# Hybrid encoder layer on one core: casts of reloaded block sums placed behind a fixed ScalarE order, earlier squares and norms in the first FFN's opening, and unordered first weight casts in the second FFN

## Chip, cores and metric

One core of a Trainium2 chip. The metric is the device time of one execution of the whole program in microseconds (us); shorter is better. Before the change it is 1978.37 us, the median of three runs (1977.86 to 1978.83).

## What is computed

One layer of a bidirectional encoder on x of 1 x 1024 x 1024 float32: a half feed-forward step, a mixer (attention beside a recurrent branch), a second half step, a last norm.

```python
def swiglu_half_step(x, gain, w_in, w_out):
    h = rms_norm(x, gain)
    gate, up = jnp.split(h @ w_in, 2, axis=-1)
    return (jax.nn.silu(gate) * up) @ w_out
...
  x = x + 1/2 * SwiGLU_1(RMSNorm(x))
  x = x + W_out [ GroupNorm_attn(GQA(...)) || HGRN2_bidir(...) ]
  x = x + 1/2 * SwiGLU_2(RMSNorm(x))
  x = RMSNorm(x)
```

D_MODEL is 1024 and D_FF is 2816, so `w_in` is 1024 x 5632. The change lies wholly in the `h @ w_in` product of the two feed-forward steps, here called FFN1 and FFN2 ("ffn1" and "ffn2" in names).

## The kernel before, in words

**Precision and blocks.** A float32 operand is split in two: a part rounded to fp32r, written by ScalarE (the "cast"), and the remainder, written by VectorE or GpSimd (the "low" of a weight, the "rest" of an activation). Each product is three matmuls: rounded by rounded, rounded by rest, rest by rounded.

`ffn_up` makes one 128-wide column group f of `w_in` at a time, 22 in all (gate and up halves together). For f = 2 and on it uses a Strassen-like scheme over half blocks (`unit` and `product`, matmuls at L311, PSUM tiles pa, pb, pc, pd). The first two groups, f = 0 and 1, are done by plain products (`plain`, matmuls at L293, tiles pp), because those need only the transposed x (operands B1 and B2, made of B11, B12 and B21, B22), while the Strassen products need block sums T1 to T4 of the transposed x as well.

**Row blocks.** x is 8 tiles of 128 rows, two to a row block i = 0 to 3. In FFN1 the last four tiles share one large tile, x_late. For each block: squares and their sums (`square`, ScalarE), the root (`root`: VectorE, then GpSimd's pow), normalisation (`norm`, VectorE), 16 transposes (`turn`, PE at L467), four casts from PSUM into B (`cast`, ScalarE), four rests (`rest`, VectorE), then block sums t1 to t4 (`sum1`, `sum2`, `sums`), which become T operands. t1 is not transformed in place: it is stored to DRAM (d_t1) and reloaded (`load_sum`, tile t1b). The reloaded t1b is written into the space of B12 by `place` (cast at L185, rest at L186), once the plain products have read B12's columns there. `place` also writes the T2 to T4 pieces of blocks 2 and 3.

**What sets the order.** Each engine runs its own queue in order. FFN1's opening has its order written out by hand: `act`, `dve` and `pool` issue each instruction behind the last one of that engine that was given in this way (all of these appear at L412, the line of the helper). Code outside it is placed by a scheduler that knows dependencies and priorities. `self.behind(x)` keeps an instruction behind x; `self.exp`, set to the last hand-ordered ScalarE instruction, is used so for the weight splits (L93, L94) of the first units. PSUM tiles share eight banks (tag "u"), so a transpose or a product also waits until the last reader of its bank is done. SyncE (SP) issues loads and stores in its queue's order.

The opening runs: blocks 0 and 1 are transposed; `plain(0)` and `plain(1)` run on columns 0 to 128 (named pp_0_0 and pp_1_0), then 128 to 256 (pp_0_128, pp_1_128), with the transposes of block 1 between the halves of the second, block 2 before and block 3 between the halves of the fourth; then both run on columns 256 to 512 (96 matmuls) over all four blocks, and unit f = 2 follows.

**FFN2's opening** has no hand order. The last attention tile pair ends in two residual additions per x tile (L1269, after the scale rs_ao). x_6 is normalised on the chip and stored; x_7 is stored to DRAM (L1275, GpSimd) as soon as it is whole and reloaded (L1516, SP), squared (L115) and normalised. `blocks(0)` transposes and casts the first block, `first(0, ...)` splits the weights of f = 0 (cast at L402, low at L404), with both kinds kept behind the last cast and rest of block 0 (`since`, `lo_since`), and `first(1, ...)` likewise. raw_in tiles are raw weights (L249).

Of the kernel before, what the change touches and what calls it, by code (L numbers as in the profile page):

```python
# [44 lines left out]
class Trunk:  # L45
# [135 lines left out]
    def place(self, dst, pt, i, lo_engine):  # L181

        ptv = pt.rearrange("p (k t) -> p k t", t=P)
        hi, lo = (dst[:, j, :, i * P : (i + 1) * P] for j in range(2))
        self.cast = self.nc.scalar.copy(hi, ptv)  # L185
        self.lo = lo_engine.tensor_sub(lo, ptv, hi.bitcast(F32))  # L186

    def ffn_up(self, name, pair, acts, comb, early_lo, mid, early, begin):
# [21 lines left out]
        def both(row):  # L210

            key = f"B{row}"
            if key not in T:
                T[key] = self.B.tile([P, 2, 2, 4, 512], F32R, name=f"{name}_{key}", tag="B")
            return T[key]
# [60 lines left out]
        def result(what, nm):  # L276
            return self.cc.tile([P, 512], F32, name=f"{what}_{name}_{nm}", tag="c")

        def plain(f, A, lo, hi, act=lambda fn, *a: fn(*a), dve=lambda fn, *a: fn(*a), between=None):

            w = hi - lo
            if begin and w == P:
                shared = self.bank(f"pp_{name}_{f}_{lo}")
                ps = [shared[:, 0 : 2 * w], shared[:, 2 * w : 4 * w]]
            else:
                ps = [self.bank(f"pp{j}_{name}_{f}_{lo}") for j in range(2)]
            halves = lambda t: t[:, : 2 * w].rearrange("p (h t) -> p h t", h=2)
            B = [both(row) for row in "12"]
            for j in range(2):
                for k in range(NK):  # L290
                    ks = slice((k % 4) * P, (k % 4 + 1) * P)
                    for i, (a, b) in enumerate(((0, 0), (0, 1), (1, 0))):
                        nc.tensor.matmul(  # L293
                            halves(ps[j]), A[2 * j + k // 4][:, a, ks],
                            B[k // 4][:, :, b, k % 4, lo:hi],
                            start=(k == 0 and i == 0), stop=(k == NK - 1 and i == 2),
                        )
                if between and not j:
                    between()
            sg = result("sg", f"{f}_{lo}")  # L300
            act(nc.scalar.activation, sg[:, : 2 * w], ps[0][:, : 2 * w], AF.Silu)
            dve(nc.vector.tensor_mul, sg[:, : 2 * w], sg[:, : 2 * w], ps[1][:, : 2 * w])
            nc.sync.dma_start(
                acts[f].rearrange("p (h t) -> p h t", h=2)[:, :, lo:hi], halves(sg)
            )
# [88 lines left out]

        A, ahead = {}, {}

        def first(f, raws, since, lo_since):
            A[f] = []
            for i in range(4):
                hl = self.wop.tile([P, 2, 512], F32R, name=f"hl_in_{name}_{f}_A{i}", tag="wop")  # L400
                with self.behind(since):
                    nc.scalar.copy(hl[:, 0, :], raws[i])  # L402
                with self.behind(lo_since):
                    early_lo.tensor_sub(hl[:, 1, :], raws[i], hl[:, 0, :].bitcast(F32))  # L404
                A[f].append(hl)

        if begin:
# [11 lines left out]
            xs, gain, gain_ps, raws = begin(raw_weights, big)  # L419
# [5 lines left out]
            def square(t, on_act=True):  # L425
                out = ss[t // 2][:, t % 2 : t % 2 + 1]
                if on_act:
                    act(nc.scalar.activation, junk[0], xs[t], AF.Square, accum_out=out)
                else:
                    dve(nc.vector.scalar_tensor_tensor, out=junk[1], in0=xs[t], scalar=1.0, in1=xs[t],  # L430
                        op0=ALU.mult, op1=ALU.mult, accum_out=out)

            def root(i, j, n):
                work = self.stat.tile([P, 2, n], F32, name=f"rs_n0_{i}_{j}", tag=f"rs{n}")
                dve(nc.vector.tensor_scalar, work[:, 0, :], ss[i][:, j : j + n], 1.0 / D, EPS,
                    ALU.mult, ALU.add)
                pool(nc.gpsimd.tensor_tensor, out=work[:, 1, :], in0=work[:, 0, :],
                     in1=self.neg_half[:, :n], op=ALU.pow)
                for m in range(n):
                    rs[2 * i + j + m] = work[:, 1, m : m + 1]  # L440

            def norm(t, cols=slice(0, D)):
                dve(nc.vector.scalar_tensor_tensor, out=xs[t][:, cols], in0=xs[t][:, cols],
                    scalar=rs[t], in1=gain[:, cols], op0=ALU.mult, op1=ALU.mult)
# [26 lines left out]
            def parts(key, i):  # L471
                return (op(key)[:, j, :, i * P : (i + 1) * P] for j in range(2))

            def cast(key, pt, i):
                hi, lo = parts(key, i)
                act(nc.scalar.copy, hi, pt.rearrange("p (k t) -> p k t", t=P))
# [25 lines left out]
            def second():  # L502
                pt, t = turn(1), sum_tiles(1)
                for k in range(4):
                    cast(keys[k], pt[k], 1)
                for k in (0, 2, 1, 3):
                    rest(keys[k], pt[k], 1)
                square(4)
                square(5)
                return pt, t  # L510

            with self.tc.high_priority():
                square(0)
                square(1)
                root(0, 0, 1)
                norm(0, lower)
                root(0, 1, 1)
                norm(0, upper)
                norm(1, lower)
                norm(1, upper)  # L520
                pts = turn(0)
                casts, lows = weight(0, raws[0])
                casts[0]()
                casts[1]()
                for k in range(4):
                    cast(keys[k], pts[k], 0)
                casts[2]()
                casts[3]()
                lows[0]()
                rest("B11", pts[0], 0)  # L530
                rest("B12", pts[2], 0)
                lows[1]()
                rest("B21", pts[1], 0)
                rest("B22", pts[3], 0)
                lows[2]()
                lows[3]()
                square(2)
                square(3)
                casts, lows = weight(1, raws[1])
                for f in casts:  # L540
                    f()
                root(1, 0, 2)
                lows[0]()
                lows[1]()
                norm(2)
                norm(3)
                lows[2]()
                lows[3]()
                t0 = sum_tiles(0)
                sum1(0, t0, pts)  # L550
                plain(0, A[0], 0, 128, act, dve)
                turned = []
                plain(1, A[1], 0, 128, act, dve, lambda: turned.append(second()))
                ptn, t1_ = turned.pop()
                root(2, 0, 2)
                norm(4)
                norm(5)
                square(6)
                square(7)
                root(3, 0, 2)  # L560
                sum2(t0, pts)
                sum1(1, t1_, ptn)
                norm(6)
                norm(7)
                plain(0, A[0], 128, 256, act, dve)
                sum2(t1_, ptn)
                third = []

                def rows(i):
                    pt = turn(i)  # L570
                    for k in range(4):
                        cast(keys[k], pt[k], i)
                        rest(keys[k], pt[k], i)
                    third.append(pt)

                rows(2)
                plain(1, A[1], 128, 256, act, dve, lambda: rows(3))
                pts, ptn = third
                for key, t in zip(("T2", "T3"), t0[1:3]):
                    cast(key, t, 0)  # L580
            cast("T4", t0[3], 0)
            for i, t in ((0, t0), (1, t1_)):
                for key, src in zip(("T2", "T3", "T4"), t[1:]):
# [8 lines left out]
        else:  # L592
            with self.tc.high_priority():
                ahead[0] = pair(0)
                raws = raw_weights(0)
# [1 line left out]
            with self.tc.high_priority():  # L597
                banks = blocks(0)
            since, lo_since = self.cast, self.lo
            first(0, raws, since, lo_since)  # L600
            plain(0, A[0], 0, 128)
            sums(0, *banks)
            banks = blocks(1)
# [10 lines left out]
        for f in range(early, NF):  # L614
            u = unit(f)
            next(u)
            self.exp = None
            if before:
                next(before)
            next(u)  # L620
            before = u
            if f - early < early:
                stored_sums(f - early)
            if f == NF // 2 and mid:
                mid()
# [961 lines left out]
```

## Time and profile before

| | |
|---|---|
| median of three runs | 1978.37 us |
| the profiled execution | 1975.92 us |
| its span, first to last instruction | 1973.9 us |
| TensorE (PE) busy | 1938.7 us, 98% of the span |
| VectorE (DVE) busy | 1256.3 us, 64% |
| ScalarE (ACT) busy | 796.7 us, 40% |
| GpSimd (POOL) busy | 763.0 us, 39% |
| mean granted TensorE clock | 0.997 |

The page of the profile gives sums over the whole span. The timeline of an engine lists its instructions in order of time, runs of the same kind merged: start, duration, engine, line, operation, output<-inputs, count, and in brackets how long the engine had stood idle before and whose end released it. Names there leave buffer numbers out (t1b_ffn, pp_ffn). The windows view gives busy time per engine in chosen stretches, with the granted clock and the DMA engines' share. L numbers are those of the kernel before; after the change they are one higher from L185 on.

### The profile page before, as it was taken

The page shows a single profiled execution, that of the slowest core. Times are in us where ns is not written, and L with a number is a line of the kernel's source. Part 1 is how long each engine was busy: PE and PEld are TensorE (multiplying, and loading weights), DVE is VectorE, ACT ScalarE, POOL GpSimd, SP SyncE. Part 2 cuts the span into 40 slices and gives each one's busy share as a digit, 9 for nine tenths or more (in the row PEclk, how much of TensorE's full clock was granted, in tenths as well). Part 3 has the DMA queues.
Part 4 walks back from the last instruction along what each step waited for, and adds up shares of the span by engine and source line. Part 5 has one row for each costly group of instructions (what it writes and reads, how often), then busy time and mean ns, then how long its engine had stood idle before and what let it go on. Part 6 is the DMA issues. An engine that isn't in the chain of part 4 may idle for free.

```text
span 1973.9 us, 26682 instructions
## 1 busy us (share of the span) xinstructions
PE 1938.7 (98%) x10233; PEld 1663.8 (84%) x10233; DVE 1256.3 (64%) x1546; ACT 796.7 (40%) x1260; POOL 763.0 (39%) x581
## 2 busy tenths in 40 slices
PE   8999999999999999999999999989999999999998
PEld 7888888887888799989899888878888888888886
DVE  7556676656976672768772556666456666657866
ACT  6333343324444432333332446654333333344344
POOL 1764645534660000041230324425555455426711
PEclk9999999999999999999999999999999999999999
DMA  8333333227775211131224352175333333158644
GB/s 249 107 123 100 103 123 101 70 97 275 250 232 171 100 33 54 33 97 29 90 87 139 123 176 76 65 239 149 126 111 96 107 102 96 68 187 316 219 122 161
DMA packets 218011, 256.70 MB, mean 130 GB/s; under 512 B 12550, under 2 KB 148762, under 8 KB 217884
## 3 DMA queue, kind: packets, MB, share of 16 engines
q1 hardware_dynamic: 208684, 224.06, 35.4%
q0 software_dynamic: 9200, 30.94, 4.1%
q8 instruction: 80, 1.31, 0.3%
q14 instruction: 47, 0.39, 0.1%
HBM read 184.17 MB, written 70.78 MB: 129 GB/s over the span
## 4 chain that ended last, share of the span: by engine, by line
PE 88%; DVE 4%; DMA 3%; issue 2%; ACT 2%; POOL 0%; SPq 0%; DVEq 0%; POOLq 0%; ACTq 0%
PE pa_ffn L311 17%; PE pd_ffn L311 11%; PE pya_ffn L700 7%; PE rec_ps L162 6%; PE pc_ffn L311 6%; PE pb_ffn L311 6%; PE pp_ffn L293 4%; PE pye_ffn L700 3%; PE pyc_ffn L700 3%; PE pyd_ffn L700 3%; PE lv L928 3%; PE ri_ps L839 2%; PE aq_ps L839 2%; PE pa L1217 2%; PE pv L1189 2%; PE s L1157 2%
## 5 line engine op out<-in xcount | busy, mean ns | idle before, releaser
L311 PE MATMUL pa_ffn<-ffn_T,hl_in_ffn_S 128*128 128x512 f32 x960 | 236.7, 389 | 0.0
L94 DVE TENSOR_TENSOR hl_in_ffn_A<-raw_in_ffn,hl_in_ffn_A 128x512 fp32r<-128x512 f32 x120 | 173.0, 1442 | 93.7 <-ACT hl_in_ffn_A L93 93.6
L311 PE MATMUL pd_ffn<-ffn_B,hl_in_ffn_S 128*128 128x512 f32 x936 | 225.6, 389 | 0.0
L311 PEld LDWEIGHTS pa_ffn<-ffn_T,hl_in_ffn_S 128*128 128x128 f32 x960 | 180.2, 188 | 37.4
L311 PEld LDWEIGHTS pd_ffn<-ffn_B,hl_in_ffn_S 128*128 128x128 f32 x936 | 175.7, 188 | 36.5
L94 DVE TENSOR_TENSOR hl_in_ffn_S<-s_ffn,hl_in_ffn_S 128x512 fp32r<-128x512 f32 x160 | 140.7, 884 | 79.6 <-ACT hl_in_ffn_S L93 79.4
L93 ACT CAST hl_in_ffn_S<-s_ffn 128x512 fp32r<-128x512 f32 x160 | 99.1, 622 | 213.6 <-PE pd_ffn L311 160.3
L93 ACT CAST hl_in_ffn_A<-raw_in_ffn 128x512 fp32r<-128x512 f32 x120 | 75.0, 626 | 139.9 <-PE pc_ffn L311 70.9
L94 DVE TENSOR_TENSOR hl_out_ffn_A<-raw_out_ffn_A,hl_out_ffn_A 128x1024 fp32r<-128x1024 f32 (+1 forms) x66 | 97.6, 1493 | 50.8 <-ACT hl_out_ffn_A L93 50.2
L94 DVE TENSOR_TENSOR hl_out_ffn_S<-raw_out_ffn_S,hl_out_ffn_S 128x512 fp32r<-128x512 f32 (+1 forms) x88 | 106.3, 1217 | 36.8 <-ACT hl_out_ffn_S L93 36.8
L267 POOL TENSOR_TENSOR s_ffn<-s_ffn,raw_in_ffn 128x512 f32<-128x512 f32 x40 | 63.5, 1588 | 165.4 <-issue 110.5
L162 PE MATMUL rec_ps<-hm,hl_rec_w 128*128 128x512 f32 x528 | 121.6, 390 | 1.9 <-DVE hm L145 1.9
L700 PE MATMUL pya_ffn<-hl_out_ffn_S 128*128 128x512 f32 x528 | 120.7, 389 | 0.4 <-DVE hl_out_ffn_S L94 0.4
L162 PEld LDWEIGHTS rec_ps<-hm,hl_rec_w 128*128 128x128 f32 x528 | 98.7, 188 | 22.4 <-DVE hm L145 2.2
L700 PEld LDWEIGHTS pya_ffn<-hl_out_ffn_S 128*128 128x128 f32 x528 | 99.0, 188 | 21.4 <-DVE hl_out_ffn_S L94 0.8
L311 PE MATMUL pa_ffn<-ffn_B,hl_in_ffn_A 128*128 128x512 f32 x480 | 116.9, 389 | 0.0
L311 PE MATMUL pc_ffn<-ffn_T,hl_in_ffn_A 128*128 128x512 f32 x480 | 115.9, 389 | 0.0
L311 PE MATMUL pb_ffn<-ffn_B,hl_in_ffn_A 128*128 128x512 f32 x480 | 115.3, 389 | 0.0
L93 ACT CAST hl_out_ffn_S<-raw_out_ffn_S 128x512 fp32r<-128x512 f32 (+1 forms) x88 | 73.3, 837 | 96.4 <-PE pya_ffn L700 40.9
L266 POOL TENSOR_TENSOR s_ffn<-raw_in_ffn 128x512 f32<-128x512 f32 x40 | 52.6, 1316 | 138.4 <-DVE hl_in_ffn_S L94 138.2
L311 PEld LDWEIGHTS pc_ffn<-ffn_T,hl_in_ffn_A 128*128 128x128 f32 x480 | 90.1, 188 | 18.7
L311 PEld LDWEIGHTS pb_ffn<-ffn_B,hl_in_ffn_A 128*128 128x128 f32 x480 | 90.1, 188 | 18.7
(295 smaller groups left out, 4018.3 us busy)
## 6 DMA issues: line engine op xcount, KB each, us to landing
raw_in_ffn<-in_ffn_w_in SPq DMA_DIRECT2D x88, 512.0 KB, 4.2
raw_out_ffn_S<-d_comb SPq DMA_DIRECT2D x88, 256.0 KB, 2.7
d_comb<-g_ffn POOLq DMA_DIRECT2D x80, 256.0 KB, 2.3
raw_out_ffn_A<-d_act SPq DMA_DIRECT2D x66, 256.0 KB, 5.2
ffn_kept<-in_ffn_w_out SPq DMA_DIRECT2D x65, 256.0 KB, 5.3
d_act<-g_ffn SPq DMA_DIRECT2D x60, 256.0 KB, 2.2
raw_out_ffn_A<-in_ffn_w_out SPq DMA_DIRECT2D x52, 256.0 KB, 5.4
x<-d_x SPq DMA_DIRECT2D x24, 512.0 KB, 4.8
```

The costliest lines, as they stand in the source:

```text
L93: nc.scalar.copy(hl[:, 0, :], src)
L94: (lo_engine or nc.vector).tensor_sub(hl[:, 1, :], src, hl[:, 0, :].bitcast(F32))
L162: nc.tensor.matmul(out, hl[:, a, ks], h[half][b][:, k, cols], start=(k == 0 and i == 0), stop=(k == NK - 1 and i == 2),)
L266: nc.gpsimd.tensor_add(s1, a21, a22)
L267: nc.gpsimd.tensor_sub(s2, s1, a11)
L293: nc.tensor.matmul(halves(ps[j]), A[2 * j + k // 4][:, a, ks], B[k // 4][:, :, b, k % 4, lo:hi], start=(k == 0 and i == 0), stop=(k == NK ...
L311: nc.tensor.matmul(ps, A[:, a, ks], op(key)[:, b, k, :], start=(first and k == 0 and i == 0), stop=(k == 3 and i == 2), skip_group_check=True,
L700: nc.tensor.matmul(ps, hl[:, a, j * P : (j + 1) * P], hl[:, b, hi], start=(first and i == 0 and n == 0), stop=(i == last and n == 2), skip ...
L839: nc.tensor.matmul(ps[:, tt, :], h[half][a][:, k, ts], hl[k // 4][:, b, ws], start=(k == 0 and i == 0), stop=(k == NK - 1 and i == 2),)
L928: nc.tensor.matmul(pl[:, cs], now[:, 0, cs], now[:, 1, cs], start=True, stop=True)
L1157: nc.tensor.matmul(ps[:, ks], qT[:, a, qs], kT[:, b, kv, ks], start=(i == 0), stop=(i == 2))
L1189: nc.tensor.matmul(ps, vt[:, j, a, vs], pT[j][:, b, i4, :], start=(st == 0 and i == 0), stop=(st == NT - 1 and i == 2),)
```

## The change

Four edits, none of which adds or removes an instruction or changes a tile, a load or a matmul in size:

1. `place` issues its cast behind `self.exp`, and `self.exp` is cleared two calls later in the loop over units.
2. `first(0, ...)` in FFN2 no longer passes `since` and `lo_since`, so the f = 0 weight casts and lows are not tied to block 0. f = 1 still passes them.
3. The squares of x tiles 4 and 5 move ahead of `plain(1)` on columns 0 to 128; root 2, norms 4 and 5, squares 6 and 7 and root 3 move into `second()`, between that product's halves.
4. The casts of T2 and T3 of block 0 move from behind block 3's casts to between block 2 and block 3.

```diff
@@ place
-        self.cast = self.nc.scalar.copy(hi, ptv)
+        with self.behind(self.exp):
+            self.cast = self.nc.scalar.copy(hi, ptv)
...
@@ first
-        def first(f, raws, since, lo_since):
+        def first(f, raws, since=None, lo_since=None):
...
@@ second
                     rest(keys[k], pt[k], 1)
-                square(4)
-                square(5)
+                root(2, 0, 2)
+                norm(4)
+                norm(5)
+                square(6)
+                square(7)
+                root(3, 0, 2)
                 return pt, t
...
                 plain(0, A[0], 0, 128, act, dve)
+                square(4)
+                square(5)
                 turned = []
                 plain(1, A[1], 0, 128, act, dve, lambda: turned.append(second()))
                 ptn, t1_ = turned.pop()
-                root(2, 0, 2)
-                norm(4)
-                norm(5)
-                square(6)
-                square(7)
-                root(3, 0, 2)
                 sum2(t0, pts)
...
                 rows(2)
+                for key, t in zip(("T2", "T3"), t0[1:3]):
+                    cast(key, t, 0)
                 plain(1, A[1], 128, 256, act, dve, lambda: rows(3))
                 pts, ptn = third
-                for key, t in zip(("T2", "T3"), t0[1:3]):
-                    cast(key, t, 0)
...
-            first(0, raws, since, lo_since)
+            first(0, raws)
...
             u = unit(f)
             next(u)
-            self.exp = None
             if before:
                 next(before)
             next(u)
+            self.exp = None
```

**ScalarE in FFN1, around the transposes of block 3.** In a name such as pt_ffn1_B12_2 the digit after B12 is the row block; t1b_ffn1_0 is the reloaded sum of block 0; sg_ffn1_1_128 is the SiLU of pp_1_128. Before:

```order
L412 CAST ffn1_B1_281<-pt_ffn1_B12_2_547 128x4x128
L185 CAST ffn1_B1_281<-t1b_ffn1_0_800 128x4x128
L412 CAST ffn1_B2_283<-pt_ffn1_B22_2_552 128x4x128
L185 CAST ffn1_B1_281<-t1b_ffn1_1_802 128x4x128
L412 CAST ffn1_B1_281<-pt_ffn1_B11_3_590 128x4x128
L412 CAST ffn1_B2_283<-pt_ffn1_B21_3_595 128x4x128
L412 CAST ffn1_B1_281<-pt_ffn1_B12_3_600 128x4x128
L230 COPY t3_ffn1_2_662<-pt_ffn1_B12_2_547 128x512
L412 CAST ffn1_B2_283<-pt_ffn1_B22_3_605 128x4x128
L412 ACTIVATE sg_ffn1_1_128_642<-pp_ffn1_1_128_565 128x256
```

After, at the same place:

```order
L413 CAST ffn1_B1_281<-pt_ffn1_B12_2_547 128x4x128
L413 CAST ffn1_B2_283<-pt_ffn1_B22_2_552 128x4x128
L413 CAST ffn1_T2_191<-t2_ffn1_0_317 128x4x128
L413 CAST ffn1_T3_566<-t3_ffn1_0_318 128x4x128
L413 CAST ffn1_B1_281<-pt_ffn1_B11_3_593 128x4x128
L231 COPY t3_ffn1_2_662<-pt_ffn1_B12_2_547 128x512
L413 CAST ffn1_B2_283<-pt_ffn1_B21_3_598 128x4x128
L413 CAST ffn1_B1_281<-pt_ffn1_B12_3_603 128x4x128
L413 CAST ffn1_B2_283<-pt_ffn1_B22_3_608 128x4x128
L413 ACTIVATE sg_ffn1_1_128_645<-pp_ffn1_1_128_568 128x256
```

The two casts of t1b have left this stretch (they now stand behind the T casts that follow it and one weight cast), two T casts of block 0 have come in, and the copy of t3_2 stands behind one cast of block 3 where it stood behind three.

**VectorE at the start of FFN2.** rs_ao3 is the scale of the last attention pair, x2_6 and x2_7 the last two x tiles, hl_in_ffn2_0_A0 to A3 the split weights of f = 0. Before:

```order
L1205 TENSOR_TENSOR ssq3_10705<-ssq3_10705,sq3_3_11216 128x256
L85 TENSOR_SCALAR rs_ao3_11249<-oss3_11246 128x2
L1269 SCALAR_TENSOR_TENSOR x2_6_11219<-pa6_11221,rs_ao3_11249,x2_6_11219 128x512 x2
L1269 SCALAR_TENSOR_TENSOR x2_7_11263<-pa7_0_11265,rs_ao3_11249,x2_7_11263 128x512
L85 TENSOR_SCALAR rs_n2_6_11258<-ss_n2_6_11256 128x1
L125 SCALAR_TENSOR_TENSOR xn_n2_6_11255<-x2_6_11219,rs_n2_6_11258,g_ffn2_norm_9012 128x1024
L1269 SCALAR_TENSOR_TENSOR x2_7_11263<-pa7_1_11279,rs_ao3_11249,x2_7_11263 128x512
```

After:

```order
L1206 TENSOR_TENSOR ssq3_10705<-ssq3_10705,sq3_3_11216 128x256
L405 TENSOR_TENSOR hl_in_ffn2_0_A0_11378<-raw_in_ffn2_0_0_11340,hl_in_ffn2_0_A0_11378 128x512
L405 TENSOR_TENSOR hl_in_ffn2_0_A1_11381<-raw_in_ffn2_0_0_11340,hl_in_ffn2_0_A1_11381 128x512
L85 TENSOR_SCALAR rs_ao3_11249<-oss3_11246 128x2
L405 TENSOR_TENSOR hl_in_ffn2_0_A2_11384<-raw_in_ffn2_0_1_11342,hl_in_ffn2_0_A2_11384 128x512
L405 TENSOR_TENSOR hl_in_ffn2_0_A3_11387<-raw_in_ffn2_0_1_11342,hl_in_ffn2_0_A3_11387 128x512
L1270 SCALAR_TENSOR_TENSOR x2_6_11219<-pa6_11221,rs_ao3_11249,x2_6_11219 128x512 x2
L1270 SCALAR_TENSOR_TENSOR x2_7_11263<-pa7_0_11265,rs_ao3_11249,x2_7_11263 128x512
L85 TENSOR_SCALAR rs_n2_6_11258<-ss_n2_6_11256 128x1
L125 SCALAR_TENSOR_TENSOR xn_n2_6_11255<-x2_6_11219,rs_n2_6_11258,g_ffn2_norm_9012 128x1024
L1270 SCALAR_TENSOR_TENSOR x2_7_11263<-pa7_1_11279,rs_ao3_11249,x2_7_11263 128x512
```

The four lows of f = 0, which before stand behind the block's rests, now stand around rs_ao3 and ahead of every residual addition of x_6 and x_7. On ScalarE the four casts likewise stand behind the last square of the attention output and ahead of the square of x_6.

**SP in FFN1, the reload of the fourth sum.** Before:

```order
L303 DMA d_act0_99<-sg_ffn1_0_256_742 256x1x256
L242 DMA t1b_ffn1_3_806<-d_t1_ffn1_189 128x512
L249 DMA raw_in_ffn1_5_1_1247<-in_ffn1_w_in 128x8x128
L249 DMA raw_in_ffn1_6_0_1387<-in_ffn1_w_in 128x8x128
L303 DMA d_act1_100<-sg_ffn1_1_256_796 256x1x256
```

After:

```order
L304 DMA d_act0_99<-sg_ffn1_0_256_742 256x1x256
L250 DMA raw_in_ffn1_5_1_1247<-in_ffn1_w_in 128x8x128
L250 DMA raw_in_ffn1_6_0_1387<-in_ffn1_w_in 128x8x128
L243 DMA t1b_ffn1_3_806<-d_t1_ffn1_189 128x512
L304 DMA d_act1_100<-sg_ffn1_1_256_796 256x1x256
```

The reload of t1b_3 now stands behind two raw weight loads, which wait until the buffers of unit 2's raw weights are free.

## Prediction

> **What bounds the kernel now.** I read the page first, then PE's timeline in the two places that the change touches, then the other engines' timelines there.
>
> ```profile
> PE 1938.7 (98%) x10233; PEld 1663.8 (84%) x10233; DVE 1256.3 (64%) x1546; ACT 796.7 (40%) x1260; POOL 763.0 (39%) x581
> PE 88%; DVE 4%; DMA 3%; issue 2%; ACT 2%; POOL 0%; SPq 0%; DVEq 0%; POOLq 0%; ACTq 0%
> ```
>
> PE is busy for 98% of a 1973.9 us span, so an order that adds no work can only win back PE's waits, 35 us in all, and stretches at a low clock. A wait on another engine counts only where PE stands behind it. In FFN1's opening PE's timeline shows:
>
> ```profile
> 33.24 1.38 PE L467 MATMUL pt_ffn_B<-ident,x_late 128*128 128x128 f32 x8 [0.32 <-DVE t_ffn L412]
> 34.56 5.42 PE L293 MATMUL pp_ffn<-ffn_B,hl_in_ffn_A 128*128 128x256 f32 x43
> 40.85 1.03 PE L467 MATMUL pt_ffn_B<-ident,x_late 128*128 128x128 f32 x8
> 44.91 1.12 PE L467 MATMUL pt_ffn_B<-ident,x_late 128*128 128x128 f32 x4 [3.02 <-ACT t_ffn L230]
> 47.84 23.81 PE L293 MATMUL pp_ffn<-ffn_B,hl_in_ffn_A 128*128 128x512 f32 x96 [1.82 <-DVE sg_ffn L412]
> 71.49 2.88 PE L311 MATMUL pa_ffn<-ffn_B,hl_in_ffn_A 128*128 128x512 f32 x12
> 74.21 1.98 PE L311 MATMUL pb_ffn<-ffn_B,hl_in_ffn_A 128*128 128x512 f32 x8
> ```
>
> The last four transposes of block 3 wait 3.02 us for the copy of t3_2, the 96 matmuls behind them 1.82 us more. The windows view adds a third loss; its columns are length, busy time of PE, PEld, DVE, ACT and POOL, granted clock, DMA share, GB/s:
>
> ```profile
> 41.40:44.83 3.43, 0.49 (x5) 0.25 (x3) 3.43 (x6) 2.54 (x5) 0.00 (x0) 1.00 0.61 222
> 44.83:51.65 6.82, 4.92 (x13) 3.78 (x14) 4.55 (x8) 5.58 (x13) 4.13 (x4) 0.50 0.16 58
> 1330.00:1333.50 3.50, 0.00 (x0) 0.00 (x0) 0.79 (x3) 2.45 (x6) 3.09 (x4) 1.00 1.09 325
> ```
>
> For 6.82 us the granted clock is 0.50, behind a 3.43 us stretch in which PE worked 0.49 us; in the third row, in FFN2, PE stands for 3.50 us and the clock is 1.00. Why the copy is late stands on ScalarE's queue:
>
> ```profile
> 38.85 0.62 ACT L185 CAST ffn_B<-t1b_ffn 128x512 fp32r<-128x512 f32 x1 [4.33 <-DMA t1b_ffn<-d_t_ffn]
> 42.29 0.62 ACT L185 CAST ffn_B<-t1b_ffn 128x512 fp32r<-128x512 f32 x1 [2.33 <-DMA t1b_ffn<-d_t_ffn]
> 42.81 1.55 ACT L412 CAST ffn_B<-pt_ffn_B 128x512 fp32r<-128x512 f32 x3
> 44.25 0.61 ACT L230 COPY t_ffn<-pt_ffn_B 128x512 f32<-128x512 f32 x1
> 46.06 0.59 ACT L412 CAST ffn_B<-pt_ffn_B 128x512 fp32r<-128x512 f32 x1 [1.21 <-PE pt_ffn_B L467]
> ```
>
> Two casts of t1b, whose results PE needs far later, hold the queue while their reloads are under way; the copy ends at 44.86 and PE goes on at 44.91.
>
> **Part 1, FFN1.** With the t1b casts out, nothing between block 2's casts and the copy waits for a load: the copy stands behind only two T casts of block 0 and the first cast of block 3, and ends before block 3's third group of transposes. The losses one by one:
>
> The 0.32 us wait at 33.24 and the stretch in that row (1.38 against 1.03 us for the same eight transposes) come from VectorE, which does norms before the sums that free the banks:
>
> ```profile
> 22.14 1.56 ACT L412 CAST ffn_B<-pt_ffn_B 128x512 fp32r<-128x512 f32 x3 [2.93 <-PE pt_ffn_B L467]
> 25.49 1.06 ACT L412 ACTIVATE ffn_T<-x_late 128x1024 fp32r<-128x1024 f32 x1
> 29.44 2.48 DVE L412 SCALAR_TENSOR_TENSOR x_late<-x_late,rs_n,g_ffn_norm 128x1024 f32<-128x1024 f32 x2 [0.81 <-POOL rs_n L412]
> L1422 SPq DMA_DIRECT2D x_late<-in_x x2: 432/2087/3742, 8.6 to 12.4; - x2
> DMA to landing us min/median/max: 6.4/7.6/8.9
> ```
>
> Squares 4 and 5 need two times 1.06 us plus a read, 2.3 us; ScalarE stands idle for 2.93 us before 22.14 and both x tiles have landed by 12.4 + 6.4 = 18.8, so they fit there with some 0.6 us to spare. If x_5 landed over 2 us later, block 1's casts and PE would wait for the excess. Norms 4 and 5 then start about 2 us before 29.44, and the sums follow sooner: 0.7 us off PE (0.32 + 0.35).
>
> The last transposes then end near 41.7: 40.85 + 1.03 + 0.5 for the last four, less 0.7. The 96 matmuls need the third of block 3's casts and its rest; as ScalarE does 0.55 us a cast and VectorE some 0.65 a rest, behind the same kind of work on the second group, the first matmul goes at about 42.0 and the others behind the rest, at 42.6. So the run of 96 starts in effect at 42.4, not 47.84: 5.4 us. At the full clock's pitch, 0.227 us (from 71.49 to 74.21 for pa's twelve of the same size), it lasts 21.9 us with the last one's tail, not 23.81: 1.9 us. It ends at 64.3 where it ended at 71.65, **7.3 us** earlier. Of this the clock has 2.4 (the 1.9, and 0.5 of the four slow transposes); the waits alone have **4.9**.
>
> Are the 2.4 to be counted? I have one profiled execution, and its rows say both: a wait of 3.02 us with 0.49 us of work around it was followed by half clock, one of 3.54 us in FFN2 was not. I take half, **1.2**, and keep 0 and 2.4 as ends. [...]
>
> What is late next? GpSimd does the T rests, and unit f = 2 waits for its weight sums:
>
> ```profile
> 47.52 8.44 POOL L412 TENSOR_TENSOR ffn_T<-t_ffn,ffn_T 128x512 fp32r<-128x512 f32 x6 [14.74 <-ACT ffn_T L412]
> 64.67 1.29 POOL L267 TENSOR_TENSOR s_ffn<-s_ffn,raw_in_ffn 128x512 f32<-128x512 f32 x1
> 62.21 0.56 SPq L242 DMA_DIRECT2D t1b_ffn<-d_t_ffn  x1
> 69.53 1.01 SPq L249 DMA_DIRECT2D raw_in_ffn<-in_ffn_w_in  x2
> ```
>
> This chain had to move too. Edit 4 lets two of the six rests run in the 14.74 us of idle time, near 37 to 41; the other four follow sg_1_128 from about 43.6 and end near 49.2, not 55.96. The s2 sum then ends near 59.2, not 65.96, and the two raw loads that hang on it go at 62.8 instead of 69.53. t1b_3, now behind them, would land at 67 to 69; with its cast and another ahead of it on ScalarE, p1's copy is done by 70.8. PE wants it 34 matmuls after 64.3, at 72.0. Cover: about 1 us. If VectorE had to stand aside for one of the two rests now beside its norms and sums, 8.44/6 = 1.4 us would go; I count nothing, since its sums and rests there read one operand from PSUM and only the norms read SBUF alone, and keep 1.4 as an end. [...]
>
> **Part 2, FFN2.** PE's, DVE's and ACT's timelines, and the x_7 store and reload:
>
> ```profile
> 1321.42 0.50 PE L293 MATMUL pp_ffn<-ffn_B,hl_in_ffn_A 128*128 128x256 f32 x2 [1.40 <-ACT hl_in_ffn_A L402]
> 1322.46 0.50 PE L293 MATMUL pp_ffn<-ffn_B,hl_in_ffn_A 128*128 128x256 f32 x2 [0.53 <-ACT hl_in_ffn_A L402]
> 1323.59 5.52 PE L293 MATMUL pp_ffn<-ffn_B,hl_in_ffn_A 128*128 128x256 f32 x44
> 1333.53 0.73 PE L293 MATMUL pp_ffn<-ffn_B,hl_in_ffn_A 128*128 128x512 f32 x2 [3.54 <-ACT ffn_B L185]
> 1312.69 0.16 DVE L85 TENSOR_SCALAR rs_ao<-oss 128x2 f32<-128x2 f32 x1 [2.80 <-PE oss L1257]
> 1313.70 1.41 DVE L1269 SCALAR_TENSOR_TENSOR x<-pa,rs_ao,x 128x512 f32<-128x512 f32 x2 [0.84 <-POOL rs_ao L86]
> 1318.37 0.74 DVE L1269 SCALAR_TENSOR_TENSOR x<-pa,rs_ao,x 128x512 f32<-128x512 f32 x1
> 1319.42 2.48 DVE L186 TENSOR_TENSOR ffn_B<-pt_ffn_B,ffn_B 128x512 fp32r<-128x512 f32 x4 [0.31 <-ACT ffn_B L185]
> 1321.82 3.69 DVE L404 TENSOR_TENSOR hl_in_ffn_A<-raw_in_ffn,hl_in_ffn_A 128x512 fp32r<-128x512 f32 x6
> 1304.19 3.07 SPq L249 DMA_DIRECT2D raw_in_ffn<-in_ffn_w_in  x2
> DMA to landing us min/median/max: 8.0/8.7/9.3
> 1319.41 0.53 POOL L1275 DMA_DIRECT2D d_x<-x  x1
> 1326.73 0.32 SPq L1516 DMA_DIRECT2D xn<-d_x  x1
> 1331.33 1.06 ACT L115 ACTIVATE junk<-xn 128x1024 f32<-128x1024 f32 x1 [1.05 <-DMA xn<-d_x]
> ```
>
> The early casts and lows remove 1.40 + 0.53 in front of the first product, but VectorE's queue now waits for the weight loads: the first was issued at 1304.2 and took 8.0 us, to 1312.2, the second at 1304.6 and took 9.3, to 1313.9. Two casts and two lows (0.6 each) put rs_ao at 1314.0, and two lows more put x_6's additions at 1315.8, 2.1 us late. x_7's second addition moves from 1318.37 to 20.5, the rests of block 0 from 1319.42 to 21.2. The first product runs freely once three rests are done, at 1323.1 instead of 1323.59: 0.4 gained.
>
> PE then stands at the 3.54 us wait as before, and its end hangs on the reload of x_7. Square, root and norm follow its landing. The cast that PE waits for stood behind T4's cast and the square and came 1.6 us after the landing; now it stands right behind the square, 0.5 sooner. But the store issues 2.2 us later, at 1321.6. Store and reload took 7.3 and 4.6 us; at the same times PE is 1.7 us worse than before. They ran beside the raw loads of f = 1, of which the second waited for x_0's transposes (1318.11) and now goes some 5 us earlier, out of the store's way; if that wins back the 2.2 us PE gains 0.5, if more, up to 2. I take **0.7 gained**, ends -1.7 and 2.
>
> **Sum.** 4.9 + 1.2 + 0.7 = 6.8 us. On the profiled execution's own 1975.92 us, with all its 2.4 us of clock, 1975.92 - 7.3 - 0.7 = 1967.9. The median of the runs is 2.45 us above that execution, and I cannot say whether they hold the slow stretch: 1978.37 - 6.8 = **1971.6**. One measurement of this kernel can tell about 0.2%, 4.0 us, so faster means below 1974.4.
>
> **Rivals.**
> - **The reload eats the FFN2 gain.** If store and reload take what they took, FFN2 costs 1.7, 1978.37 - 4.9 - 1.2 + 1.7 = 1974.0, without the clock's part 1975.2. For it: the store takes 7.3 us, so the queues are full. Against: the loads ahead of it move up. Chance 0.2.
> - **Unit f = 2 gives it back.** t1b_3 lands after 70 because the two raw loads ahead of it were issued late; ScalarE's cast of it blocks p1's copy and PE waits at pa's second product, 1 to 3 us: 1972.6 to 1974.6. For it the 1 us of cover; against, PE has no wait there now. Chance 0.12.
> - **Slower.** The residual additions now stand behind a weight load. Each us that raw_0_1 lands after 1313.9 delays x_6, x_7, the store, the reload and so PE by one. At 1321 all is eaten; past 1325, over 20 us from its issue, the kernel is slower by over 4 us, 1982.4. It took 9.3 us here. Chance 0.05.
> - **Nothing moves.** ScalarE's new waits land elsewhere in the hand order (squares 4 and 5 held by an x_5 that lands past 21). 1978.4. Chance 0.05.
>
> **Numbers.** My forecast, 0.58, has its own range of 1968.8 to 1973.2. The range reaches to 1975.2, the first rival's end. Faster: 0.58, half of the first rival and three quarters of the second: 0.77; same 0.18; slower 0.05.
>
> **What would show it.** In the changed profile: no t1b cast on ScalarE between 33 and 46; no PE wait over 1 us before the 96 matmuls, and a full clock from 44 to 52; the 96 matmuls over by 64.3; squares 4 and 5 before 22; s2 before 60; p1's copy before 72. In FFN2, the four weight casts ahead of x_6's square, no PE wait for hl_in_ffn_A, and one wait of 2 to 4 us for the cast behind x_7's square. A wait in unit 2, or FFN2 losing over 2 us, would make it wrong.

## The result and the profile after

The changed kernel takes 1971.93 us (median of 7 runs, 1970.28 to 1974.96) against 1978.59 us (7 runs beside them): the ratio is 0.9966, 95% interval 0.9955 to 0.9978, so 6.7 us or 0.34% faster. The forecast was 1971.6. The profiled execution takes 1972.17 us with a span of 1970.2. Two executions below, one of before (5221.65 us) and one of experiment 4 (2783.60 us), lie far outside all others and are left out of all ratios and spreads.

PE's timeline in FFN1's opening, after:

```profile
32.37 1.91 PE L468 MATMUL pt_ffn_B<-ident,x_late 128*128 128x128 f32 x16
34.03 5.15 PE L294 MATMUL pp_ffn<-ffn_B,hl_in_ffn_A 128*128 128x256 f32 x41
40.30 1.47 PE L468 MATMUL pt_ffn_B<-ident,x_late 128*128 128x128 f32 x12
42.06 0.50 PE L294 MATMUL pp_ffn<-ffn_B,hl_in_ffn_A 128*128 128x512 f32 x1 [0.29 <-ACT ffn_B L413]
42.90 21.83 PE L294 MATMUL pp_ffn<-ffn_B,hl_in_ffn_A 128*128 128x512 f32 x95 [0.33 <-DVE ffn_B L413]
64.56 2.88 PE L312 MATMUL pa_ffn<-ffn_B,hl_in_ffn_A 128*128 128x512 f32 x12
72.27 2.88 PE L312 MATMUL pa_ffn<-ffn_T,hl_in_ffn_S 128*128 128x512 f32 x12
```

The waits of 3.02 and 1.82 us are gone, 0.29 and 0.33 are left, and 95 of the 96 matmuls last 21.8 us at full clock (the granted clock is 1.00 from 38.00 to 71.50). ScalarE's timeline shows why, and how little cover unit f = 2 has:

```profile
20.76 1.06 ACT L413 ACTIVATE ffn_T<-x_late 128x1024 fp32r<-128x1024 f32 x1
22.62 1.56 ACT L413 CAST ffn_B<-pt_ffn_B 128x512 fp32r<-128x512 f32 x3 [0.71 <-PE pt_ffn_B L468]
40.14 0.59 ACT L231 COPY t_ffn<-pt_ffn_B 128x512 f32<-128x512 f32 x1
45.24 1.17 ACT L186 CAST ffn_B<-t1b_ffn 128x512 fp32r<-128x512 f32 x2
70.36 0.62 ACT L186 CAST ffn_B<-t1b_ffn 128x512 fp32r<-128x512 f32 x1 [5.45 <-DMA t1b_ffn<-d_t_ffn]
71.41 0.58 ACT L362 COPY p_ffn<-pa_ffn 128x512 f32<-128x512 f32 x1
```

Square 5 ends 0.7 us before the casts of block 1 can start; the copy of t3_2 ends at 40.73, before PE asks for its bank; the casts of t1b follow at 45.24. The last reload lands at 70.36, p1's copy ends at 71.99 and PE takes pa up again at 72.27: 0.3 us of cover.

FFN2's opening, after: PE, then VectorE, GpSimd's store of x_7, SP's reload, its square and the cast behind it.

```profile
1311.84 1.91 PE L177 MATMUL pt_ffn_B<-ident,xn 128*128 128x128 f32 x16
1316.86 5.77 PE L294 MATMUL pp_ffn<-ffn_B,hl_in_ffn_A 128*128 128x256 f32 x46 [0.53 <-DVE ffn_B L187]
1328.19 0.83 PE L294 MATMUL pp_ffn<-ffn_B,hl_in_ffn_A 128*128 128x512 f32 x2 [4.68 <-ACT ffn_B L186]
1307.84 0.15 DVE L85 TENSOR_SCALAR rs_ao<-oss 128x2 f32<-128x2 f32 x1
1309.61 2.06 DVE L1270 SCALAR_TENSOR_TENSOR x<-pa,rs_ao,x 128x512 f32<-128x512 f32 x3
1315.32 0.53 POOL L1276 DMA_DIRECT2D d_x<-x  x1
1321.45 0.32 SPq L1517 DMA_DIRECT2D xn<-d_x  x1
1326.52 1.06 ACT L115 ACTIVATE junk<-xn 128x1024 f32<-128x1024 f32 x1 [3.69 <-DMA xn<-d_x]
1327.58 0.56 ACT L186 CAST ffn_B<-pt_ffn_B 128x512 fp32r<-128x512 f32 x1
```

Block 0's transposes (1318.11 before) come 6.27 us earlier. Against them, the first product resumes 0.46 us earlier than before, x_7's store is issued 2.18 us later, its reload lands 1.46 us later, and the product of f = 1 starts 0.93 us later, behind a wait of 4.68 instead of 3.54 us. The windows view adds two stretches of half clock that the profile of before did not have (columns as in the prediction):

```profile
1171.67:1175.08 3.41, 1.23 (x8) 0.93 (x7) 2.58 (x4) 3.23 (x5) 0.09 (x1) 1.00 0.58 239
1175.08:1178.49 3.41, 3.41 (x14) 2.87 (x12) 3.03 (x3) 2.02 (x5) 1.47 (x1) 0.50 0.00 0
1325.27:1328.68 3.41, 0.48 (x2) 0.44 (x3) 0.66 (x2) 2.16 (x5) 0.56 (x1) 1.00 1.11 320
1328.68:1332.09 3.41, 3.41 (x14) 2.97 (x12) 3.41 (x4) 3.41 (x7) 3.35 (x2) 0.50 0.93 276
```

Each costs, by an estimate from its length, about 1.7 us of PE's work (half of 3.41). Of the 6.93 us that this execution is ahead at pa (71.49 to 64.56), 3.7 are left at its end (span 1973.9 to 1970.2); the medians are 6.7 apart. Single executions of the changed kernel differ by 4.7 us, and profiles alone do not rank kernels here; the experiments are read by stages.

### The profile page after: what moved, and what is told of

Its sections match the earlier page's. It is cut to its first block, busy times and chain, and to the rows that moved or that the text cites. A ratio compares the mean times of both kernels' runs of the same rounds, so it can differ in the third digit from the quotient of the medians.

```text
span 1970.2 us, 26692 instructions
## 1 busy us (share of the span) xinstructions
PE 1939.4 (98%) x10233; PEld 1665.0 (85%) x10233; DVE 1254.3 (64%) x1546; ACT 796.2 (40%) x1260; POOL 758.5 (38%) x581
## 4 chain that ended last, share of the span: by engine, by line
PE 92%; DVE 3%; DMA 2%; ACT 1%; issue 1%; POOL 0%; SPq 0%; DVEq 0%; POOLq 0%; ACTq 0%
PE pa_ffn L312 17%; PE pd_ffn L312 11%; PE pya_ffn L701 9%; PE rec_ps L162 6%; PE pc_ffn L312 6%; PE pb_ffn L312 6%; PE pp_ffn L294 4%; PE pye_ffn L701 3%; PE pyd_ffn L701 3%; PE pyc_ffn L701 3%; PE pyb_ffn L701 3%; PE lv L929 3%; PE ri_ps L840 2%; PE aq_ps L840 2%; PE pv L1190 2%; PE s L1158 2%
```

## The experiments

Two stage lengths, from the same instructions in every profile, carry the comparison. "FFN1" runs from the start of block 2's transposes to the start of pa (before: 31.88 to 71.49), "FFN2" from the start of block 0's transposes to the first matmul of f = 1's product (before: 1318.11 to 1333.53). Each ratio is to runs of before beside that kernel, with medians of 1978.59 us for the changed kernel, 1978.48 for 1 to 4, 1978.65 for 5 to 8 and 1979.65 for 9.

| kernel | median us | ratio to before, 95% interval | FFN1 us | FFN2 us |
|---|---|---|---|---|
| before | 1978.59 | | 39.61 | 15.42 |
| changed | 1971.93 | 0.9966, 0.9955 to 0.9978 | 32.19 | 16.35 |
| 1: first-FFN edits only | 1970.63 | 0.9961, 0.9948 to 0.9974 | 32.21 | 15.44 |
| 2: second-FFN edit only | 1980.24 | 1.0012, 1.0003 to 1.0021 | 40.99 | 16.48 |
| 3: changed, lows late | 1964.89 | 0.9934, 0.9921 to 0.9947 | 32.19 | 10.62 |
| 4: `place` edit only | 1974.67 | 0.9983, 0.9973 to 0.9992 | 37.97 | 15.43 |
| 5: changed, x_7's square held | 1969.79 | 0.9950, 0.9936 to 0.9965 | 32.20 | 11.93 |
| 6: as 1, x_7's square held | 1967.86 | 0.9941, 0.9926 to 0.9956 | 32.19 | 13.38 |
| 7: changed without edit 3 | 1972.36 | 0.9967, 0.9954 to 0.9980 | 33.82 | 16.02 |
| 8: changed without edit 4 | 1974.50 | 0.9977, 0.9967 to 0.9987 | 35.04 | 16.24 |
| 9: T cast edit (4) only | 1974.01 | 0.9973, 0.9962 to 0.9985 | 38.96 | 13.61 |

**1. The second FFN's edit undone.**

```diff
-            first(0, raws)
+            first(0, raws, since, lo_since)
```

> The changed kernel with the second FFN's first weight casts and lows tied behind block 0 again, as before. Theory: the early lows cost FFN2's opening about 1 us in waits, because they delay x_7's store by 2.2 us; without them the kernel should be about 1 us faster than the changed one (near 1971 where the changed one has 1972), its FFN1 as in the changed kernel (the 96 matmuls over at 64.3 to 64.8), the wait for x_7's reload back at 3.5 us. Rival, my forecast's term: the early casts gain 0.7 us, so that undoing them makes it 0.7 us slower than the changed kernel.

FFN2's length is back at 15.44 us, 0.9 less than in the changed kernel, and FFN1 is the same: so the edit costs 0.9 us in waits, as the theory had it, and the rival (a gain of 0.7) falls. By time alone the intervals of the two kernels overlap.

**2. The second FFN's edit alone.**

```diff
-        def first(f, raws, since, lo_since):
+        def first(f, raws, since=None, lo_since=None):
...
-            first(0, raws, since, lo_since)
+            first(0, raws)
```

> The kernel before with only the second FFN's first weight casts and lows untied. Theory: about 1 us slower than before (1979.5), with x_7's store issued 2.2 us later against the transposes of block 0 and the wait for its reload at 4.5 to 4.7 us; FFN1 as before, the wait of 3.0 us with its half clock or without it. Rival: 0.7 us faster than before (1977.9).

It is slower than before, by an interval that leaves out 1. PE's timeline in FFN2, and in FFN1, where nothing was changed:

```profile
48.13 24.92 PE L293 MATMUL pp_ffn<-ffn_B,hl_in_ffn_A 128*128 128x512 f32 x96 [1.82 <-DVE sg_ffn L412]
1337.95 1.22 PE L293 MATMUL pp_ffn<-ffn_B,hl_in_ffn_A 128*128 128x512 f32 x2 [4.87 <-ACT ffn_B L185]
```

The wait is 4.87 us, 0.2 above what was expected. In FFN1 the 96 matmuls took 24.92 us where before's profile has 23.81: 1.1 us more behind nearly the same waits (3.28 and 1.82 us). That half clock lasted longer there is an estimate from this time: experiment 4 has the same 24.92 us with a granted clock of 0.50 for the first 6.2 of them, before has it for the first 3.8.

**3. Casts early, lows late.**

```diff
-            first(0, raws)
+            first(0, raws, None, lo_since)
```

> The changed kernel with the f = 0 casts of the second FFN still free, but their lows behind block 0's rests, as before. Theory: VectorE's residual additions and x_7's store come at their old times, ScalarE's casts are done early; FFN2's opening is 0 to 1 us better than with the casts tied, and the kernel 1 to 2 us faster than the changed one (near 1970.5). Rival: ScalarE's queue, which now waits for the weight loads ahead of x_6's square, is what delays the store; then nothing is won against the changed kernel.

This is the fastest kernel of the study: 1964.89 us (5 runs, 1963.99 to 1965.87), 13.6 us under the 1978.48 of before's runs beside it and 7.0 under the changed kernel; the intervals of its ratio and the changed kernel's do not meet. Against the changed kernel that is far more than the 1 to 2 us that the theory allowed, so the theory missed something. PE's timeline and ScalarE's in its FFN2:

```profile
1312.95 0.51 PE L294 MATMUL pp_ffn<-ffn_B,hl_in_ffn_A 128*128 128x256 f32 x2 [0.40 <-ACT ffn_B L186]
1315.09 1.70 PE L294 MATMUL pp_ffn<-ffn_B,hl_in_ffn_A 128*128 128x256 f32 x12 [0.52 <-DVE hl_in_ffn_A L405]
1321.26 6.41 PE L294 MATMUL pp_ffn<-ffn_B,hl_in_ffn_A 128*128 128x512 f32 x26
1317.95 0.58 ACT L186 CAST ffn_B<-pt_ffn_B 128x512 fp32r<-128x512 f32 x1
1321.54 0.59 ACT L186 CAST ffn_B<-pt_ffn_B 128x512 fp32r<-128x512 f32 x1 [1.31 <-PE pt_ffn_B L177]
1323.88 1.06 ACT L115 ACTIVATE junk<-xn 128x1024 f32<-128x1024 f32 x1 [1.76 <-DMA xn<-d_x]
```

PE does not wait at 1321.26 at all. The two last casts of block 1 (1317.95 and 1321.54) now stand ahead of x_7's square; in the changed kernel (1327.58 above) and before they stand behind it, and so behind the reload of x_7. Before, where the square starts at 1331.33 and PE goes on at 1333.53:

```profile
1332.90 1.07 ACT L185 CAST ffn_B<-pt_ffn_B 128x512 fp32r<-128x512 f32 x2
```

PE never needed x_7 there: it needed a cast that was queued behind it. Experiment 5 tests this by itself.

**4. The `place` edit alone.**

```diff
-        self.cast = self.nc.scalar.copy(hi, ptv)
+        with self.behind(self.exp):
+            self.cast = self.nc.scalar.copy(hi, ptv)
```

(and `self.exp` cleared later, as in the change).

> The kernel before with only the first edit: casts of the reloaded sums behind the fixed order. Theory: the 3.0 and 1.8 us waits go (the 96 matmuls over by 65.0 to 65.5), but GpSimd's first T rests start 7 us later than in the changed kernel, so that the weight sums of unit 2 and the reload of the fourth sum are 2 to 3 us later and PE waits 2 to 3 us in unit 2: 3 us faster than before in all (1975.5). Rival: edit 4 is not needed, no wait in unit 2, 5 to 6 us faster than before (1973).

The time is near the theory's, but the waits are those of neither account. PE's timeline:

```profile
42.77 0.66 PE L468 MATMUL pt_ffn_B<-ident,x_late 128*128 128x128 f32 x4 [0.73 <-ACT t_ffn L231]
45.24 24.92 PE L294 MATMUL pp_ffn<-ffn_B,hl_in_ffn_A 128*128 128x512 f32 x96 [1.82 <-DVE sg_ffn L413]
77.71 2.88 PE L312 MATMUL pa_ffn<-ffn_T,hl_in_ffn_S 128*128 128x512 f32 x12
```

The 3.02 us wait fell to 0.73, but the 1.82 us ahead of the 96 matmuls stayed, the half clock too (granted clock 0.50 from 44.60 to 51.43), and in unit 2 (77.71) PE did not wait: the theory's 2 to 3 us there did not come.

**5 and 6. x_7's square held behind block 1's last cast**, in the changed kernel and in experiment 1's:

```diff
             banks = blocks(1)
+            self.block1 = self.cast
...
+            with self.behind(self.hold):
                 self.nc.scalar.activation(
                     junk[:, cols], x[:, cols], AF.Square, accum_out=ss[:, i : i + 1]
                 )
...
+                        k.hold = k.block1
                         k.norm_rows(xt, gain2, xt, f"n2_{t}", junk=junk)
+                        k.hold = None
```

> The changed kernel with one thing more: the square of x_7 in the second FFN is kept behind the last cast of row block 1 on ScalarE. Theory: PE's wait in FFN2's opening (4.7 us in the changed kernel) was never for x_7 itself but for casts of block 1 that stood behind its square on ScalarE's queue; with the square behind them the wait falls below 1 us, though x_7's store is as late as in the changed kernel, and the kernel comes to about 1966. Rival: the early lows and the late store are what costs; then the wait only moves to the transposes of x_7's block and the kernel stays near 1971.

> The first experiment's kernel (first-FFN edits alone, second FFN's weight casts tied as before) with the same hold on x_7's square. Theory: as the order of the square against block 1's casts is all that was gained by leaving the lows late, this comes to 1965 to 1966.5, within 1.5 us of the version with early casts and late lows (1964.9), the 3.5 us wait gone and the 1.4 + 0.5 us waits in front of the first product still there. Rival: the early casts themselves gave the gain; then it stays near 1970.5.

PE's rows of 5, then of 6:

```profile
1325.65 0.73 PE L297 MATMUL pp_ffn<-ffn_B,hl_in_ffn_A 128*128 128x512 f32 x2 [0.24 <-ACT ffn_B L189]
1342.61 5.66 PE L297 MATMUL pp_ffn<-ffn_B,hl_in_ffn_A 128*128 128x256 f32 x45 [1.41 <-ACT t_ffn L234]
```

```profile
1316.05 0.50 PE L297 MATMUL pp_ffn<-ffn_B,hl_in_ffn_A 128*128 128x256 f32 x2 [1.40 <-ACT hl_in_ffn_A L406]
1326.12 0.73 PE L297 MATMUL pp_ffn<-ffn_B,hl_in_ffn_A 128*128 128x512 f32 x2 [1.51 <-ACT ffn_B L189]
```

In 5 the wait falls from 4.68 to 0.24 us, which shows the queue order as its cause. FFN2's length falls by 4.4 us, the time only by 2.1. Of the rest, 1.6 us go into waits of 0.63 and 1.41 us for ScalarE behind this stage, where the changed kernel has 0.45. Another 1.8 us were lost in the first FFN up to its second product (from the start of pa to that of pyc 474.99 us, 473.19 in the changed kernel), away from anything that was edited, which I did not follow. In 5 the eight transposes behind the wait take 1.03 us and the next 46 matmuls 10.72 us, in the changed kernel, where the granted clock is 0.50 from 1328.68 to 1332.09, 1.91 and 11.52. So 5 does not have the half clock that took 1.7 us there, and this sum leaves 2.7 us. In 6 the wait falls to 1.5 us. 6 misses its range (1965 to 1966.5) by 1.4 us. In FFN2's length it stands halfway: 15.44 us in 1, 13.38 here, 10.62 in 3. So, from experiment 1 on, the order of the square gives 2.1 us of what 3 won, and the other 2.8 go with the early casts (1.40 us here ahead of the first product, 0.40 in 3; no wait ahead of f = 1's product in 3, 1.5 here). From the changed kernel on, the order gives 4.4 of 5.7 us, and the rest goes with the late lows.

**7. Without the squares edit (3).** The squares, norms and roots stand where they stood before (the `second` and `plain` hunks of the diff undone).

> The changed kernel without its third edit (squares, roots and norms where they were). Theory, the prediction's term: PE's 0.3 us wait ahead of block 2's transposes is back with its stretch, the 96 matmuls end 0.7 us later against the opening's start than in the changed kernel, 1972.6 in all, which the time alone cannot tell. Rival: the norms in their old place push the sums back by more, so that block 3's transposes wait too, 2 us or more.

```profile
42.76 0.66 PE L468 MATMUL pt_ffn_B<-ident,x_late 128*128 128x128 f32 x4 [0.73 <-ACT t_ffn L231]
43.69 22.32 PE L294 MATMUL pp_ffn<-ffn_B,hl_in_ffn_A 128*128 128x512 f32 x96 [0.27 <-DVE t_ffn L232]
```

FFN1 is 1.6 us longer, not 0.7: besides the 0.3 us wait ahead of block 2's third transposes and its stretch, the copy of t3_2 comes 0.73 us late for the last ones. The time cannot tell it, as expected.

**8 and 9. Edit 4 taken out, and alone.**

```diff
-                for key, t in zip(("T2", "T3"), t0[1:3]):
-                    cast(key, t, 0)
                 plain(1, A[1], 128, 256, act, dve, lambda: rows(3))
                 pts, ptn = third
+                for key, t in zip(("T2", "T3"), t0[1:3]):
+                    cast(key, t, 0)
```

> The changed kernel without its fourth edit (T2 and T3 of block 0 cast behind block 3's casts again). Theory: GpSimd's six first rests start near 43 and end 2 us later than in the changed kernel, the weight sum s2 and the two raw loads come 2 us later, the reload of the fourth sum lands near 72.5 and PE waits about 2 us in unit 2: 1974. Rival: the copy is 1 us sooner without the two casts ahead of it and the chain has cover; no wait in unit 2, 1971 to 1972.

> The kernel before with only the fourth edit (T2 and T3 of block 0 cast between block 2 and block 3). Theory: the fourth edit does not serve GpSimd's chain; it lets the 96 matmuls start in a PSUM bank whose last reader is the sum t1_2 and not the product with sg_1_128, so that the 1.8 us wait ahead of them goes, while the 3.0 us wait for the copy stays, because the casts of the reloaded sums are still in the queue: 1.5 to 2 us faster than before (1976.8). Rival: the wait ahead of the 96 goes only together with the first edit; then it stays at 1.8 us, and the kernel at 1978.6.

GpSimd's and PE's rows of 8:

```profile
43.12 8.88 POOL L413 TENSOR_TENSOR ffn_T<-t_ffn,ffn_T 128x512 fp32r<-128x512 f32 x6 [12.34 <-ACT ffn_T L413]
61.16 1.29 POOL L268 TENSOR_TENSOR s_ffn<-s_ffn,raw_in_ffn 128x512 f32<-128x512 f32 x1
58.16 1.46 SPq L243 DMA_DIRECT2D t1b_ffn<-d_t_ffn  x1
43.67 23.65 PE L294 MATMUL pp_ffn<-ffn_B,hl_in_ffn_A 128*128 128x512 f32 x96 [2.14 <-DVE sg_ffn L413]
74.86 2.88 PE L312 MATMUL pa_ffn<-ffn_T,hl_in_ffn_S 128*128 128x512 f32 x12
```

The weight sum s2 is 2.2 us later than in the changed kernel (62.45 against 60.25), and PE still does not wait in unit 2: without edit 4 the reload of t1b_3 stands ahead of the raw loads again (58.16). What comes back is the wait ahead of the 96 matmuls, 2.14 us, for the product with sg_1_128. The time agrees with the expected 1974, for another reason than the one given. In 9, PE's rows of both stages:

```profile
46.20 24.88 PE L293 MATMUL pp_ffn<-ffn_B,hl_in_ffn_A 128*128 128x512 f32 x96 [0.70 <-DVE t_ffn L231]
1333.52 0.73 PE L293 MATMUL pp_ffn<-ffn_B,hl_in_ffn_A 128*128 128x512 f32 x2 [0.24 <-ACT ffn_B L185]
```

The wait ahead of the 96 is 0.70 and its releaser the sum t1_2: with edit 4 the 96 matmuls no longer wait for the product with sg_1_128. In 9 they start at 46.20, ahead of that product, whose SiLU ends at 46.41; in the changed kernel at 42.06, also ahead of it:

```profile
44.55 0.41 DVE L413 TENSOR_TENSOR sg_ffn<-sg_ffn,pp_ffn 128x256 f32<-128x256 f32 x1
```

That holds in every profile: with edit 4 this wait is 0.7 us or less, without it (before, 2, 4, 8) 1.8 to 2.1. As these matmuls use nothing that the product makes, another PSUM bank for their tile is the likely reason; the profiles do not list banks, so that part is inferred.

Against before's runs beside it, 9 is 5.6 us faster where 1.5 to 2 were expected. In the profiles FFN1 gives 0.65 of this and FFN2, which the edit doesn't touch, 1.8, although half clock took 1.5 us of it (granted clock 0.50 from 1325.39 to 1328.80; 44 matmuls take 7.01 us, before 5.52): there the scheduler put one cast of block 1 ahead of x_7's square, and the wait for it fell to 0.24 us. The other 3 us are not accounted for; both profiled executions lie off their medians (before's 1975.92, 9's 1976.05).

## Why the prediction was right, and where it was not

**FFN1, the main term, was right in sum.** With all of the clock's 2.4 us, 7.3 us were expected, and the stage is 7.4 shorter (39.61 to 32.19). The 96 matmuls end 32.36 us after block 2's transposes began, forecast 32.4 (64.3 less 31.88). With the half clock taken out (2.4 us of before's stage; in 4 and 9 the 3 us that the 96 matmuls took over 21.9), the parts are: edit 1 alone 2.3 us, edit 4 alone 1.2, and the changed kernel without edit 3 is 1.6 longer; together 5.1, where the waits were forecast at 4.9 and the whole stage shows 5.0 (37.2 to 32.19).

**Why the 1.82 us went was wrong.** The prediction let the 96 matmuls wait for casts and rests only and took the bank for free. The wait went through edit 4 (experiments 8 and 9), which the prediction valued for GpSimd's chain ("This chain had to move too"). That step failed: in 4 and 8 the six rests start at 43 to 45 and PE does not wait in unit 2. Edit 3's term was too small, 0.7 against 1.6, since it also brought the copy of t3_2 forward.

**Half of the clock's 2.4 us was the wrong count.** In before's profile FFN1's wait of 3.02 us has 6.82 us of half clock behind it, in 9 a wait of 2.88 us is followed by a mean granted clock of 0.57 from 44.6 to 50, and in 4 waits of 0.73 and 1.82 us have 6.83 us of half clock behind them. The 96 matmuls took 23.81 us in before, 24.92 in 2 (wait of 3.28 us) and 4, 24.88 in 9 and 23.65 in 8 (2.14). In the others, with waits under 0.8 us, 96 took 22.32 us (7) or 95 took 21.8. So in these executions the whole 2.4 belonged to the sum.

**FFN2's term had the wrong sign.** Step by step: the first product 0.4 us earlier (measured 0.46), the store 2.2 us later (2.18), the cast right behind the square; but only 0.7 us of the store's delay came back (store and reload took 11.2 us, not 11.9), and the forecast gain of 0.7 is a loss of 0.93, between my value and the first rival's 1.7. In this execution half clock behind the longer wait (0.50 from 1328.68 to 1332.09) took 1.7 us more, a term that I had not counted. With it, FFN2's opening up to the 256-wide products behind its last transposes (1318.11 to 1348.68 before, 1311.84 to 1344.97 after) is 2.6 us longer, past the 2 us that the prediction named as a sign against it. In experiment 1's execution the old wait (3.56 us) had half clock behind it as well (0.50 from 1327.59 to 1331.00). The deeper error is one of reading: the row [3.54 <-ACT ffn_B L185] names a cast of block 1, and the prediction followed the square ahead of it in ScalarE's queue to the reload and took the reload for the bound. It is the same fault that it had just described for the casts of t1b in FFN1.

**So the sum held in part by errors that cancel**: 1.2 too little for the clock in FFN1, 1.6 too much for FFN2. That the total lies 0.3 us from the median is luck. The rest of the program gave and took about 1 us at a time: waits at the mixer's start shrank from 1.93 to 0.84 us, one in attention grew from 1.49 to 2.19 us and had half clock behind it (0.50 from 1175.08 to 1178.49). Rivals: unit 2 did not give it back, but its cover was 0.3 us, not 1, as t1b_3 landed at 70.36 and not by 69. The end of 1.4 us for VectorE beside GpSimd's two early rests did not come either: its norms were over at 35.48, the rests began at 35.65, and two sums beside them took 1.28 us (35.73), as two did before with GpSimd idle (37.15). VectorE's rests of t1b, which read no PSUM, did take longer beside GpSimd before: 0.69 and 0.68 us with GpSimd idle (39.51 and 43.11), 3.48 us for two beside its weight sums (73.40). The slower side did not come: the second weight load took 9.4 us, against 20 needed. Of the other signs, s2 ended at 60.25 and not before 60, the first t1b cast stood at 45.24 and not behind 46, and FFN2's wait, 4.68 us, left its range of 2 to 4.

## What to carry to other kernels

Where an engine waits for an instruction, look at what stands ahead of that instruction in its queue before asking what it computes: twice here PE waited (3.02 and 3.54 us) for a copy or a cast that could have run microseconds earlier, but stood behind another instruction that waited for a reload. Moving work forward on one engine (the casts, on an idle ScalarE) may win what moving its partner on another (the lows, ahead of the additions on VectorE) loses, so such edits are worth splitting. And an edit in one stage can reorder another through the scheduler (experiment 9), so read the order of the whole program before crediting a gain to the edit.

## What the hardware showed that I had not expected

Half clock followed some of PE's waits and not others, and neither the longer wait nor the smaller share of work tells which. Rows of experiment 4 (FFN1), of before and of experiment 9 (both FFN2), each with the stretch behind it:

```profile
41.19:44.60 3.41, 1.51 (x12) 1.03 (x10) 2.97 (x5) 2.71 (x7) 0.00 (x0) 1.00 0.80 228
44.60:51.43 6.83, 6.18 (x15) 4.86 (x16) 5.67 (x8) 5.60 (x12) 6.51 (x5) 0.50 0.32 96
```

```profile
1328.24:1331.66 3.42, 1.74 (x16) 1.50 (x14) 2.40 (x5) 1.46 (x3) 1.81 (x2) 1.00 1.04 353
1331.66:1335.07 3.41, 1.54 (x11) 1.41 (x12) 1.72 (x3) 3.41 (x8) 2.48 (x3) 1.00 1.13 329
1335.07:1338.48 3.41, 3.41 (x17) 2.79 (x16) 3.41 (x6) 0.88 (x2) 0.00 (x0) 1.00 1.13 320
```

```profile
1321.98:1325.39 3.41, 1.63 (x12) 1.43 (x13) 3.41 (x6) 3.41 (x8) 0.00 (x0) 1.00 1.02 267
1325.39:1328.80 3.41, 3.41 (x19) 3.41 (x18) 3.41 (x7) 2.97 (x6) 0.00 (x0) 0.50 1.04 412
```

In 4 two waits of 0.73 and 1.82 us, with 1.51 us of PE's work in the 3.41 us up to 44.60, were followed by 6.83 us of half clock. In before a single wait of 3.54 us was not: PE worked 1.74 us in the first row and 1.54 in the second, and the granted clock is 1.00 in both and in the one behind them. In 9 a row with 1.63 us of work, more than those 1.54, was followed by half clock. So were rows with 0.48 and 1.23 us in the changed kernel, with 0.49 in before's FFN1, with 0.74 in experiment 1 (1324.18 to 1327.59) and with none in 7 (1324.82 to 1328.24), while before's 3.50 us without any (1330.00 to 1333.50) were not. What makes this difference is not shown here, and each row is one execution: whether FFN1's half clock is in every execution of before, no run shows.

The stretches of half clock differ between the profiled executions, which may be one reason why runs of before spread over 7 us (1975.63 to 1982.65) and the five of experiment 3, whose profiled run has a mean granted clock of 0.999, over 1.9. The granted clock on record for each run bears it out in part. In experiment 2 the time follows it (1978.2 to 1979.8 us at 0.997, 1980.2 to 1981.5 at 0.996, 1982.0 to 1983.8 at 0.995), but runs of before at 0.997 alone spread from 1975.63 to 1981.14. That the stretches cause the spread is argued from these, not tried.
